# One ring tile, a combined load of the 5th and 6th tile, and a first tile stored in 8 and 24 KB pieces, in a contrast kernel

## The chip, the cores and the metric

The kernel runs on one core of a Trainium2 chip. The metric is device time in microseconds (us); lower is better. Most executions of one kernel agree within 0.3%. Positions in time are counted from the start of the profiled span, which is shorter than the device time by 2.2 us in most runs.

## The reference

The reference takes 48 images of 512 x 512 float32 values. It moves each image away from its own mean and clips:

```python
x: (16, 3, 512, 512) float32, factor = 1.5
mean = np.mean(x, axis=(2, 3), keepdims=True)
return np.clip(mean + factor * (x - mean), 0, 1)
```

Every value is read once and written once: 50.33 MB in, 50.33 MB out.

## The kernel before

The data are cut into 12 tiles of 128 rows of 32 KB (4 MB each, four images). A tile is loaded, summed (VectorE takes 4352 columns, ScalarE the other 3840), the sums become a bias by two small matmuls, and the tile is clipped in place, ScalarE then VectorE. SP (SyncE) issues the loads, ScalarE the stores, each into its own queue. A DMA has landed when its last byte is reported in place; the report goes to a semaphore, a counter that an engine waits for. Six buffers hold tiles, so the 7th tile is loaded when the first one has been stored.

```python
CHUNKS = (5120, 3072)
FIRST = (2048, 3072, 3072)
...
xpool = ctx.enter_context(tc.tile_pool(name="xpool", bufs=BUFS))      # BUFS = 6
...
def load(t):
    xt = xpool.tile([P, ROW], f32, name="xt")
    nc.sync.dma_start(out=xt, in_=dram(x_f, t))
    tiles[t] = xt

def compute(t):
    xt = tiles[t]
    ...                                     # sums on VectorE and ScalarE, matmuls, bias
    chunks, pieces = (FIRST, True) if t == 0 else (CHUNKS, False)
    c, done = 0, 0
    for n in chunks:
        part = xt[:, c : c + n]
        nc.scalar.activation(out=part, in_=part, func=Act.Relu, bias=bias, scale=factor)
        nc.vector.tensor_scalar(out=part, in0=part, scalar1=1.0, scalar2=None, op0=Alu.min)
        if pieces and c > 0:
            store(t, done, c)
            done = c
        c += n
    store(t, done, ROW)
...
for t in range(min(BUFS, n_tiles)):
    load(t)
for t in range(n_tiles):
    compute(t)
    if t + BUFS < n_tiles:
        load(t + BUFS)
```

The first tile leaves in three stores of 8, 12 and 12 KB per row; every other tile leaves in one store.

Of the kernel before, what the change touches and what calls it, by code (L numbers as in the profile page):

```python
# [1 line left out]

# [4 lines left out]


P = 128  # L10
ROW = 8192
BUFS = 6
CHUNKS = (5120, 3072)
FIRST = (2048, 3072, 3072)
SUM = 4352


@with_exitstack
def kernel(
    ctx: ExitStack,  # L20
    tc: tile.TileContext,
    x: bass.AP,
    factor: float,
    out: bass.AP,
):


    nc = tc.nc
    f32 = mybir.dt.float32
    Alu = mybir.AluOpType  # L30
    Act = mybir.ActivationFunctionType

    B, C, H, W = x.shape
    n_img, n_pix = B * C, H * W
    ppi = n_pix // ROW
    per_tile = P // ppi
    n_tiles = n_img // per_tile
    assert ppi * ROW == n_pix and per_tile * n_tiles == n_img

    factor = float(factor)  # L40
    wconst = (1.0 - factor) / float(n_pix)

    x_f = x.rearrange("b c h w -> (b c h w)")
    out_f = out.rearrange("b c h w -> (b c h w)")

    def dram(ap, t, c0=0, c1=ROW):
        return bass.AP(tensor=ap.tensor, offset=t * P * ROW + c0, ap=[[ROW, P], [1, c1 - c0]])

    consts = ctx.enter_context(tc.tile_pool(name="consts", bufs=1))
    xpool = ctx.enter_context(tc.tile_pool(name="xpool", bufs=BUFS))  # L50
    jpool = ctx.enter_context(tc.tile_pool(name="jpool", bufs=1))
    rpool = ctx.enter_context(tc.tile_pool(name="rpool", bufs=2))
    bpool = ctx.enter_context(tc.tile_pool(name="bpool", bufs=2))
    psum = ctx.enter_context(tc.tile_pool(name="psum", bufs=2, space=bass.MemoryType.PSUM))

    blockw = consts.tile([P, P], f32, name="blockw")
    nc.gpsimd.memset(blockw, 0.0)  # L57
    for a in range(0, P, ppi):
        nc.gpsimd.memset(blockw[a : a + ppi, a : a + ppi], wconst)  # L59

    tiles = {}

    def load(t):
        xt = xpool.tile([P, ROW], f32, name="xt")
        nc.sync.dma_start(out=xt, in_=dram(x_f, t))  # L65
        tiles[t] = xt

    def compute(t):
        xt = tiles[t]
        sums = rpool.tile([P, 2], f32, name="sums")  # L70
        nc.vector.tensor_reduce(  # L71
            out=sums[:, 0:1], in_=xt[:, 0:SUM], axis=mybir.AxisListType.X, op=Alu.add
        )
        junk = jpool.tile([P, ROW - SUM], f32, name="junk")
        nc.scalar.activation(  # L75
            out=junk, in_=xt[:, SUM:ROW], func=Act.Copy, accum_out=sums[:, 1:2]
        )
        pbias = psum.tile([P, 1], f32, name="pbias")
        nc.tensor.matmul(pbias, blockw, sums[:, 1:2], start=True, stop=False)  # L79
        nc.tensor.matmul(pbias, blockw, sums[:, 0:1], start=False, stop=True)  # L80
        bias = bpool.tile([P, 1], f32, name="bias")
        nc.vector.tensor_copy(out=bias, in_=pbias)  # L82

        chunks, pieces = (FIRST, True) if t == 0 else (CHUNKS, False)
        c, done = 0, 0
        for n in chunks:
            part = xt[:, c : c + n]
            nc.scalar.activation(out=part, in_=part, func=Act.Relu, bias=bias, scale=factor)  # L88
            nc.vector.tensor_scalar(out=part, in0=part, scalar1=1.0, scalar2=None, op0=Alu.min)  # L89
            if pieces and c > 0:  # L90
                store(t, done, c)
                done = c
            c += n
        store(t, done, ROW)

    def store(t, c0, c1):
        nc.scalar.dma_start(out=dram(out_f, t, c0, c1), in_=tiles[t][:, c0:c1])  # L97

    with tc.manual_schedule():
        for t in range(min(BUFS, n_tiles)):  # L100
            load(t)
        for t in range(n_tiles):
            compute(t)
            if t + BUFS < n_tiles:
                load(t + BUFS)


# [1 line left out]
_INS = ['x', 'factor']  # L109
_OUTS = [((16, 3, 512, 512), 'float32')]  # L110

_NUMBERS = {'factor': 1.5}


# [26 lines left out]
```

## Time and profile before

| | before |
|---|---|
| device time, median of 3 | 239.76 us (239.71 to 239.78) |
| span of the profile | 237.4 us |
| DMA: loads and stores, share of 16 engines | 49.6% + 49.2% |
| busy: ScalarE, VectorE | 55%, 47% |
| one tile on the compute engines | 14.6 us |
| last store issued | 210.1 us |

From the page of the kernel before: span, busy time of the engines, the two DMA rows of the 40 slices, and the DMA queues (packets, MB, share of 16 engines' span).

```profile
span 237.4 us, 310 instructions
PE 14.0 (6%) x48; PEld 12.0 (5%) x48; DVE 111.9 (47%) x49; ACT 131.1 (55%) x50; POOL 0.9 (0%) x9
...
DMA  7999998989999999999999999999999999999996
GB/s 265 442 442 442 420 446 374 472 384 455 453 425 409 409 436 442 442 442 442 442 442 425 436 398 421 442 442 442 442 442 436 442 425 392 425 442 442 442 442 265
...
q1 hardware_dynamic: 1728, 50.33, 49.6%
q10 hardware_dynamic: 2016, 50.33, 49.2%
```

The DMA row is 9 almost everywhere and the two queues add up to 98.8%: between the first packet and the last the 16 DMA engines hardly rest (by the packet records 0.1 us of 234.3), while both compute engines are idle about half of the time. One caution in reading the second row: a slice is 5.9 us long and 16 engines start a 32 KB packet nearly together, so a slice usually counts five such rounds, 442 GB/s, and sometimes four or six. The rate over 100 us and more is 431 to 433 GB/s.

The packet records of the trace give the size of each packet. One row of a tile is one packet: 32 KB in 1.213 us, 12 KB in 0.460 us, 8 KB in 0.309 us. 3072 packets of 1.213 us over 16 engines are 232.9 us, which is the floor for this form of transfer. The other 6.9 us of the 239.76 are, from the trace of before: 2.3 us outside the span (the median less the span of the profile), 1.8 us to the first packet, 1.2 us of slower packets and 1.3 us after the last packet, with small change.

From the timeline of before, the starts of the reductions of the 5th, 6th and 12th tile, and the last store (columns: start, duration, engine, line, operation, and in brackets the idle time before it and what ended it).

```profile
71.73 4.68 DVE L71 TENSOR_REDUCE sums<-xt 128x1 f32<-128x4352 f32 x1
86.36 4.68 DVE L71 TENSOR_REDUCE sums<-xt 128x1 f32<-128x4352 f32 x1
...
195.38 4.69 DVE L71 TENSOR_REDUCE sums<-xt 128x1 f32<-128x4352 f32 x1 [4.63 <-DMA xt<-in_x_dram]
...
210.11 0.34 ACTq L97 DMA_DIRECT2D out_dram<-xt  x1
```

Tiles follow each other on the compute engines at 14.6 us where they need not wait for data, and at about 19.4 us later, which is the time the DMA needs for one load and one store of 4 MB. At 210.1 us the last store is issued, but its first packet starts at 225.9 us in the packet records: older stores are ahead of it for 15.8 us. That number is the slack of the compute engines at the end.

One more line, from the waits of the DMA-issuing queue of before (total, times, longest, in us): SP could not issue the sixth load (at 22.77 us) before the second had landed (22.75 us): in the trace both count on the same semaphore.

```profile
SPq L65 <- DMA xt<-in_x_dram: 19.6, 1, 19.6
```

### The profile page before, as it was taken

What the parts mean: (1) busy time and instruction counts of PE and PEld (TensorE: products, weight loads), DVE (VectorE), ACT (ScalarE), POOL (GpSimd) and SP (SyncE); (2) the same over time, 40 slices, a digit from 0 to 9 for tenths busy, and PEclk for the clock granted to TensorE, in tenths of its full rate; (3) what the DMA queues carried; (4) which work ended last, traced back from release to release, by engine and by line L of the source; (5) the groups of instructions that cost most, each with busy time, mean ns of one, the idle gap of its engine ahead of it and who ended that gap; (6) DMA issues with size and microseconds to landing.
All of it is one profiled execution on the core that took longest, in us unless ns stands there. A gap on an engine that the chain in (4) does not pass through costs nothing.

```text
span 237.4 us, 310 instructions
## 1 busy us (share of the span) xinstructions
PE 14.0 (6%) x48; PEld 12.0 (5%) x48; DVE 111.9 (47%) x49; ACT 131.1 (55%) x50; POOL 0.9 (0%) x9
## 2 busy tenths in 40 slices
PE   0000010100101001010010010001001001000000
PEld 0000010100101001010010010001001001000000
DVE  0072855919468293782664372552734627330000
ACT  2058678586775967769279059256536806900000
POOL 1000000000000000000000000000000000000000
DMA  7999998989999999999999999999999999999996
GB/s 265 442 442 442 420 446 374 472 384 455 453 425 409 409 436 442 442 442 442 442 442 425 436 398 421 442 442 442 442 442 436 442 425 392 425 442 442 442 442 265
DMA packets 3745, 100.67 MB, mean 424 GB/s; under 512 B 416, under 2 KB 416, under 8 KB 416
## 3 DMA queue, kind: packets, MB, share of 16 engines
q1 hardware_dynamic: 1728, 50.33, 49.6%
q10 hardware_dynamic: 2016, 50.33, 49.2%
q14 instruction: 1, 0.01, 0.0%
HBM read 50.33 MB, written 50.33 MB: 424 GB/s over the span
## 4 chain that ended last, share of the span: by engine, by line
DMA 39%; another core or an unknown queue 24%; DVE 12%; ACT 10%; issue 2%; PE 1%; SPq 0%; ACTq 0%
DMA xt<-in_x_dram 19%; DMA out_dram<-xt 19%; ACT xt L88 9%; DVE xt L89 6%; DVE sums L71 5%; ACT junk L75 1%; PE pbias L80 1%; SPq L65 0%; PE pbias L79 0%; DVE bias L82 0%; ACTq L97 0%; ACTq L88 0%; ACTq L75 0%
## 5 line engine op out<-in xcount | busy, mean ns | idle before, releaser
L88 ACT ACTIVATE xt<-xt,bias 128x3072 f32<-128x3072 f32 (+2 forms) x25 | 87.9, 3563 | 21.0 <-DVE bias L82 13.7
L89 DVE TENSOR_SCALAR xt<-xt 128x3072 f32<-128x3072 f32 (+2 forms) x25 | 54.3, 2208 | 56.1 <-ACT xt L88 56.1
L71 DVE TENSOR_REDUCE sums<-xt 128x1 f32<-128x4352 f32 x12 | 56.2, 4683 | 33.9 <-DMA xt<-in_x_dram 33.9
L75 ACT ACTIVATE junk<-xt 128x3840 f32<-128x3840 f32 x12 | 40.8, 3402 | 55.4 <-DMA xt<-in_x_dram 41.9
L79 PE MATMUL pbias<-sums,blockw 128*128 128x1 f32 x24 | 7.0, 361 | 183.8 <-ACT junk L75 183.8
L79 PEld LDWEIGHTS pbias<-sums,blockw 128*128 128x128 f32 x24 | 6.0, 311 | 184.7 <-ACT junk L75 168.0
L80 PE MATMUL pbias<-sums,blockw 128*128 128x1 f32 x24 | 7.0, 362 | 2.9 <-DVE sums L71 2.5
L80 PEld LDWEIGHTS pbias<-sums,blockw 128*128 128x128 f32 x24 | 6.0, 312 | 3.9 <-DVE sums L71 3.4
L82 DVE COPY bias<-pbias 128x1 f32<-128x1 f32 x12 | 1.9, 158 | 8.2 <-PE pbias L80 8.2
L75 ACT ACTIVATION_READ_ACCUMULATOR junk<-xt 128x1 f32 x12 | 2.2, 186 | 0.0
L75 ACT ACT_TABLE_LOAD x1 | 1.3, 1283 | 0.7 <-PEq L122 0.7
L59 POOL MEMSET blockw<- 32x32 f32 x4 | 0.5, 117 | 0.2
L57 POOL MEMSET blockw<- 128x128 f32 x1 | 0.2, 204 | 0.3 <-POOLq L122 0.3
L122 POOL MEMSET const-bfloat16-1.0<- 128x1 bf16 x1 | 0.1, 111 | 0.0
L122 POOL MEMSET const-uint8-127<- 128x1 uint8 x1 | 0.1, 111 | 0.0
L122 POOL MEMSET const-float32-1.0<- 128x1 f32 x1 | 0.1, 108 | 0.0
L122 POOL MEMSET const-float32-0.0<- 128x1 f32 x1 | 0.1, 103 | 0.2 <-issue 0.2
## 6 DMA issues: line engine op xcount, KB each, us to landing
xt<-in_x_dram SPq DMA_DIRECT2D x12, 4096.0 KB, 33.9
out_dram<-xt ACTq DMA_DIRECT2D x11, 4096.0 KB, 50.6
out_dram<-xt ACTq DMA_DIRECT2D x2, 1536.0 KB, 31.1
out_dram<-xt ACTq DMA_DIRECT2D x1, 1024.0 KB, 15.5
```

The lines of the kernel that those rows point to most:

```text
L57: nc.gpsimd.memset(blockw, 0.0)
L59: nc.gpsimd.memset(blockw[a : a + ppi, a : a + ppi], wconst)
L71: nc.vector.tensor_reduce(out=sums[:, 0:1], in_=xt[:, 0:SUM], axis=mybir.AxisListType.X, op=Alu.add)
L75: nc.scalar.activation(out=junk, in_=xt[:, SUM:ROW], func=Act.Copy, accum_out=sums[:, 1:2])
L79: nc.tensor.matmul(pbias, blockw, sums[:, 1:2], start=True, stop=False)
L80: nc.tensor.matmul(pbias, blockw, sums[:, 0:1], start=False, stop=True)
L82: nc.vector.tensor_copy(out=bias, in_=pbias)
L88: nc.scalar.activation(out=part, in_=part, func=Act.Relu, bias=bias, scale=factor)
L89: nc.vector.tensor_scalar(out=part, in0=part, scalar1=1.0, scalar2=None, op0=Alu.min)
L122: nc = _bacc.Bacc("TRN2", target_bir_lowering=False, num_devices=1)
```

## The change

The six buffers become one tile with six places, so that one DMA can fill two of them. The 5th and 6th tile are loaded by one such DMA. The first tile is stored in two pieces, 8 and 24 KB per row, instead of three. The aim is fewer DMAs and fewer waits on reused semaphores.

```diff
-    xpool = ctx.enter_context(tc.tile_pool(name="xpool", bufs=BUFS))
+    xpool = ctx.enter_context(tc.tile_pool(name="xpool", bufs=1))
...
+    ring = xpool.tile([P, BUFS, ROW], f32, name="ring")
-    def load(t):
-        xt = xpool.tile([P, ROW], f32, name="xt")
-        nc.sync.dma_start(out=xt, in_=dram(x_f, t))
-        tiles[t] = xt
+    def load(t, c0=0, c1=ROW, n=1):
+        b = t % BUFS
+        src = bass.AP(
+            tensor=x_f.tensor,
+            offset=t * P * ROW + c0,
+            ap=[[ROW, P], [P * ROW, n], [1, c1 - c0]],
+        )
+        nc.sync.dma_start(out=ring[:, b : b + n, c0:c1], in_=src)
...
-            if pieces and c > 0:
-                store(t, done, c)
-                done = c
+            if t == 0 and c == FIRST[0]:
+                store(t, 0, c)
             c += n
-        store(t, done, ROW)
+        store(t, FIRST[0] if t == 0 else 0, ROW)
...
-        for t in range(min(BUFS, n_tiles)):
-            load(t)
+        load(0)
+        load(1)
+        load(2)
+        load(3)
+        load(4, n=2)
```

More of the change, by code (lines that the diff above doesn't have):

```diff
@@ L59 @@
         nc.gpsimd.memset(blockw[a : a + ppi, a : a + ppi], wconst)
-    tiles = {}
-    def load(t):
-        xt = xpool.tile([P, ROW], f32, name="xt")
-        nc.sync.dma_start(out=xt, in_=dram(x_f, t))
-        tiles[t] = xt
+    ring = xpool.tile([P, BUFS, ROW], f32, name="ring")
[7 more added lines that the diff above has]
+        nc.sync.dma_start(out=ring[:, b : b + n, c0:c1], in_=src)
     def compute(t):
-        xt = tiles[t]
+        xt = ring[:, t % BUFS, :]
         sums = rpool.tile([P, 2], f32, name="sums")
@@ L82, in compute @@
         nc.vector.tensor_copy(out=bias, in_=pbias)
-        chunks, pieces = (FIRST, True) if t == 0 else (CHUNKS, False)
-        c, done = 0, 0
-        for n in chunks:
+        c = 0
+        for n in FIRST if t == 0 else CHUNKS:
             part = xt[:, c : c + n]
@@ L89, in compute @@
             nc.vector.tensor_scalar(out=part, in0=part, scalar1=1.0, scalar2=None, op0=Alu.min)
-            if pieces and c > 0:
-                store(t, done, c)
-                done = c
+            if t == 0 and c == FIRST[0]:
+                store(t, 0, c)
             c += n
-        store(t, done, ROW)
+        store(t, FIRST[0] if t == 0 else 0, ROW)
     def store(t, c0, c1):
-        nc.scalar.dma_start(out=dram(out_f, t, c0, c1), in_=tiles[t][:, c0:c1])
+        nc.scalar.dma_start(out=dram(out_f, t, c0, c1), in_=ring[:, t % BUFS, c0:c1])
     with tc.manual_schedule():
-        for t in range(min(BUFS, n_tiles)):
-            load(t)
+        load(0)
[3 more added lines that the diff above has]
+        load(4, n=2)
         for t in range(n_tiles):
```

## The prediction

> **What bounds it now.** The 16 DMA engines. In the table of queues the loads (q1) take 49.6% and the stores (q10) 49.2% of 16 engines' span: 98.8% of 237.4 us is 234.6 us. In the 40 slices the DMA row is 9 in nearly all; only the first and last slice move less (265 GB/s against about 442). The trace's packets are one row each: 32 KB in 1.213 us, the 12 KB pieces in 0.460, the 8 KB pieces in 0.309. 3072 rows of 32 KB over 16 engines are 232.9 us: that is the floor, and 239.76 us lies 6.9 us above it, almost all of it launch, first packet and last receipt. ACT is busy 55%, DVE 47%; one tile costs them 14.6 us in series (starts of the reduction in the timeline), while a load and a store of a tile cost the DMA about 19.4 us.
>
> **What the change does.**
> 1. One ring instead of six buffers: same bytes, same instruction order; no work added.
> 2. Loads 5 and 6 as one DMA. No load reuses a semaphore then, so SP's 19.6 us wait for load 2 (waits of the DMA queue) goes. The load queue was not empty meanwhile, so this is worth nothing. But both tiles are released together, only when 8 MB have landed.
> 3. First tile stored as 8 + 24 KB instead of 8 + 12 + 12: 128 data packets fewer. A 24 KB packet should take about 0.91 us (estimate from 0.460 for 12 KB), which saves 0.1 us in all.
>
> The Trainium skill, "DMA: Bandwidth & Descriptors", section "Queues, rings and completion order", says each engine takes turns between its queues packet by packet. This trace agrees: in the second third of the span load and store packets are about equal in number. So a 24 KB piece gets more of the engine beside 32 KB loads than two 12 KB ones: the first tile's store should land about 10 us sooner (51 instead of 62 us), and loads later. Estimate by stepping such turns with the durations above (it reproduces before's landings to about 2 us): tile 5 becomes ready at 85 to 90 us instead of 60, so its reduction starts at 85 to 90 instead of 71.7: ACT and DVE idle there some 15 us. Compute then catches up (14.6 against 19.4 us), the last load lands at about 202 to 206 instead of 195 us, and the last store is issued at 217 to 221 instead of 210 us.
>
> **Critical path.** None of it, as long as either queue has packets: two earlier stores, over 5 us of work (before: about 17), are still queued when the last store is issued.
>
> **Prediction: 239.5 us, 8 times in 10 between 238.9 and 240.3.** Faster by over 2%: 0.02; within 2%: 0.94; slower by over 2%: 0.04.
>
> **What would show it.** DMA share again 98 to 99%, all middle slices 9; q10 with 144 packets fewer, q1 with 16 fewer; a new DMA wait of 10 to 18 us before the reduction of the 5th tile, none before the 6th; first store pieces landing near 51 us; SP's 19.6 us wait gone; last store issued later, landing at the same time.
>
> **What would make it wrong.** If the combined load uses fewer than 16 engines or smaller packets; if the later release of tile 5 lets both queues run dry together (an idle slice); if the last store comes after the backlog is gone (each us late is a us lost); if piece sizes change the packet rate more than I count.

## The result, and the profile after

| | before | after |
|---|---|---|
| device time, median of 6 | 239.77 us (239.71 to 240.00) | 239.66 us (239.51 to 240.13) |
| span of the profile | 237.4 us | 237.8 us |
| DMA shares, loads + stores | 49.6% + 49.2% | 49.7% + 49.1% |
| 5th tile's reduction starts | 71.7 us | 87.5 us |
| last store issued | 210.1 us | 218.9 us |

The ratio is 0.9997, 95% interval 0.9984 to 1.001: the two are the same.

The same lines of the page, for the kernel after:

```profile
span 237.8 us, 306 instructions
PE 14.0 (6%) x48; PEld 12.0 (5%) x48; DVE 111.8 (47%) x49; ACT 131.1 (55%) x50; POOL 0.9 (0%) x9
...
DMA  7999999999999999999999999999999999999996
GB/s 265 441 441 441 416 447 375 419 456 440 441 408 425 425 425 441 441 441 441 436 436 441 425 419 425 419 442 441 441 441 430 436 441 430 419 430 419 436 441 265
...
q1 hardware_dynamic: 1712, 50.33, 49.7%
q10 hardware_dynamic: 1872, 50.33, 49.1%
```

The load queue has 16 packets fewer and the store queue 144 fewer. The 16 are the completion packets of one load (one per engine); the 144 are 128 rows and 16 completions of one store. The bytes and the shares are what they were. That exactly 16 are gone also shows that the combined load still runs on 16 engines.

From the timeline of after, the reductions of the 5th, 6th and 12th tile and the last store:

```profile
87.54 4.68 DVE L77 TENSOR_REDUCE sums<-ring 128x1 f32<-128x4352 f32 x1 [15.70 <-DMA ring<-in_x_dram]
102.17 4.68 DVE L77 TENSOR_REDUCE sums<-ring 128x1 f32<-128x4352 f32 x1
...
204.17 4.69 DVE L77 TENSOR_REDUCE sums<-ring 128x1 f32<-128x4352 f32 x1 [4.64 <-DMA ring<-in_x_dram]
...
218.91 0.34 ACTq L100 DMA_DIRECT2D out_dram<-ring  x1
```

VectorE sits idle for 15.7 us until the combined load has landed, starts the 6th tile right behind the 5th, and issues the last store 8.8 us later than before. None of it reaches the time: the first packet of the last store starts at 226.0 us (225.9 before), because older stores were still being moved until then. The wait of SP for a load is gone from the waits of its queue, where only the waits for stores are left:

```profile
SPq L72 <- DMA out_dram<-ring: 149.2, 7, 36.1
```

From the DMA issues of after (size, median us from issue to landing):

```profile
ring<-in_x_dram SPq DMA_DIRECT2D x1, 8192.0 KB, 84.8
out_dram<-ring ACTq DMA_DIRECT2D x1, 3072.0 KB, 28.3
```

The 24 KB piece was issued at 28.0 us, so the first tile's store landed at 56.3 us. The 7th load, which waits for it, was issued at 56.4 us after against 64.4 us before.

### The profile page after: what moved, and what is told of

Its sections match the earlier page's. It is cut to its first block, busy times and chain, and to the rows that moved or that the text cites. A ratio compares the mean times of both kernels' runs of the same rounds, so it can differ in the third digit from the quotient of the medians. Undisturbed runs are those within 1.5% of the kernel's fastest.

```text
span 237.8 us, 306 instructions
## 1 busy us (share of the span) xinstructions
PE 14.0 (6%) x48; PEld 12.0 (5%) x48; DVE 111.8 (47%) x49; ACT 131.1 (55%) x50; POOL 0.9 (0%) x9
## 3 DMA queue, kind: packets, MB, share of 16 engines
q1 hardware_dynamic: 1712, 50.33, 49.7%
q10 hardware_dynamic: 1872, 50.33, 49.1%
## 4 chain that ended last, share of the span: by engine, by line
DMA 42%; DVE 22%; ACT 17%; another core or an unknown queue 7%; PE 2%; issue 2%; ACTq 0%; SPq 0%
DMA ring<-in_x_dram 26%; DMA out_dram<-ring 16%; ACT ring L92 14%; DVE ring L93 12%; DVE sums L77 9%; ACT junk L81 3%; PE pbias L86 2%; PE pbias L85 0%; DVE bias L88 0%; ACTq L100 0%; ACTq L92 0%; ACTq L81 0%; SPq L72 0%
## 5 line engine op out<-in xcount | busy, mean ns | idle before, releaser
L92 ACT ACTIVATE ring<-ring,bias 128x3072 f32<-128x3072 f32 (+2 forms) x25 | 87.9, 3564 | 21.4 <-DVE bias L88 12.5
L93 DVE TENSOR_SCALAR ring<-ring 128x3072 f32<-128x3072 f32 (+2 forms) x25 | 54.3, 2208 | 56.1 <-ACT ring L92 56.1
L77 DVE TENSOR_REDUCE sums<-ring 128x1 f32<-128x4352 f32 x12 | 56.2, 4681 | 42.8 <-DMA ring<-in_x_dram 42.8
L81 ACT ACTIVATE junk<-ring 128x3840 f32<-128x3840 f32 x12 | 40.8, 3402 | 63.8 <-DMA ring<-in_x_dram 48.2
L81 ACT ACTIVATION_READ_ACCUMULATOR junk<-ring 128x1 f32 x12 | 2.2, 186 | 0.0
```

What stands on the lines that cost most here:

```text
L77: nc.vector.tensor_reduce(out=sums[:, 0:1], in_=xt[:, 0:SUM], axis=mybir.AxisListType.X, op=Alu.add)
L81: nc.scalar.activation(out=junk, in_=xt[:, SUM:ROW], func=Act.Copy, accum_out=sums[:, 1:2])
```

## The experiments

The theory is that the time is the work of the DMA engines from first to last packet. What the change does to the moments at which tiles become ready is free as long as one of the two queues has a packet. The rivals are that gains and losses of the parts cancel, and that late tiles do cost time but by an amount hidden in something else. Eleven kernels were run; every result was correct. Where a loss is read below, its interval lies well clear of 1.

### Each part alone

`e1_ring_only`: the ring with six single loads and three pieces.

```diff
-            if t == 0 and c == FIRST[0]:
-                store(t, 0, c)
+            if t == 0 and c > 0:
+                store(t, done, c)
+                done = c
             c += n
-        store(t, FIRST[0] if t == 0 else 0, ROW)
+        store(t, done, ROW)
...
-        load(4, n=2)
+        load(4)
+        load(5)
```

> The ring alone: six single loads, first tile in 8 + 12 + 12 KB as before. Theory (the time is the DMA engines' packet work, and no part of the change touches it): 239.7 us, trace like before: SP's wait of about 19.6 us for load 2 is back, last store issued at about 210 us, no DMA wait before the 5th tile. Rival (a gain of one part is cancelled by a loss of another): at least one of the three runs with one part alone differs from before by 1 us or more, and two of them in opposite directions.

Measured: 239.65 us against 239.62 us of before on that chip; ratio 1.0004 (0.9989 to 1.0019). SP's wait for a load is back (19.4 us), the 5th reduction starts at 71.6 us, the last store is issued at 210.2 us. The single tile as such changes nothing.

`e2_pair_only`: the changed kernel with the store half of that edit alone (three pieces, the combined load kept).

> Ring and combined load, three pieces. Theory: 239.7 us; the 5th tile's reduction starts at 78 to 80 us (71.7 before), since the first tile's store lands near 62 us as before and the loads get their larger share; the 6th follows 14.6 us later; the slack at the end comes back: last load at about 195 us and last store issued at about 210 us. So the lost slack at the end belongs to the pieces, not to the combined load. Rival: the late release of the 5th tile costs time, 1 us or more above before.

Measured: 239.69 us; ratio 1.0003 (0.9988 to 1.0018). From its timeline:

```profile
77.87 4.68 DVE L77 TENSOR_REDUCE sums<-ring 128x1 f32<-128x4352 f32 x1 [5.87 <-DMA ring<-in_x_dram]
...
209.15 0.34 ACTq L101 DMA_DIRECT2D out_dram<-ring  x1
```

The combined load holds the 5th tile up by 5.9 us (its start is 0.1 us before the expected 78 to 80), and the last store is issued 1.0 us earlier than before.

`e3_pieces_only`: the changed kernel with the load half of that edit alone (single loads, 8 + 24 KB).

> Ring and 8 + 24 KB pieces, loads single. Theory: 239.6 us; first tile's store lands near 54 us; the 5th tile's reduction is not held up (about 72 us), the 6th waits for its load until about 87 us; last store issued at about 219 us as in the changed kernel, which shows that the pieces alone move the end. Rival: the fewer, larger packets gain 1 us or more below before.

Measured: 239.63 us; ratio 1.0002 (0.9987 to 1.0017). From its timeline, the reduction of the 6th tile and the last store:

```profile
88.63 4.69 DVE L77 TENSOR_REDUCE sums<-ring 128x1 f32<-128x4352 f32 x1 [2.25 <-DMA ring<-in_x_dram]
...
219.92 0.34 ACTq L100 DMA_DIRECT2D out_dram<-ring  x1
```

The pieces alone delay the later loads and the end: the last store is issued at 219.9 us, the 5th tile is not held up (71.7 us). So the two parts act in different places. The 15.7 us gap of the changed kernel is the combined load on top of loads that the pieces have slowed. And since all three variants are nominally within 0.05% of before, with intervals of 0.15% (0.4 us) to each side, no part has an effect of the 1 us that the rival asked for, and there is nothing of that size to cancel. The rival falls.

### How much slack the end has

The last tile gets one or two more reductions of its own columns, whose results nobody uses (4.68 us each, on VectorE ahead of the real one):

```diff
+        if t == n_tiles - 1:
+            for _ in range(1):          # 2 in the other three kernels
+                spare = rpool.tile([P, 1], f32, name="spare")
+                nc.vector.tensor_reduce(
+                    out=spare, in_=xt[:, 0:SUM], axis=mybir.AxisListType.X, op=Alu.add
+                )
         nc.vector.tensor_reduce(
             out=sums[:, 0:1], in_=xt[:, 0:SUM], axis=mybir.AxisListType.X, op=Alu.add
         )
```

`e4_after_tail1`: the changed kernel with one.

> The changed kernel with one more reduction of 4.68 us on the last tile's path. Theory: the last store is issued 4.7 us later (at about 223.6 us) and still finds about 1 us of older stores queued (in the changed kernel the first packet of the last store started at 226.0 us, 7.1 us after its issue): 239.7 us, at most 0.5 us longer. Rival (the end of the last tile's work is on the critical path): 4.7 us longer.

`e5_after_tail2`: the changed kernel with two.

> The same with two more reductions (9.4 us). Theory: the slack of 5 to 6 us is used up, 243 to 244 us, with a gap in the DMA row just before the last store's packets. Rival (on the critical path): 249.1 us. Rival (never matters): 239.7 us.

`e6_before_tail2`: the kernel before with two.

> The kernel before with the same two reductions (9.4 us). Theory: its slack is about 14 us (last store issued at 210.1 us, its first packet at 225.9 us), so 239.8 us, no change; the change has thus spent some 9 us of hidden slack that its time does not show. Rival: the same loss as in the changed kernel.

`e7_pair_tail2`: the combined load with three pieces, and two.

> Ring and combined load with three pieces, and the two reductions. Theory (the pieces, not the combined load, took the slack): 239.8 us, no change. Rival (the combined load took it): 243 to 244 us as in the changed kernel.

| kernel | last store issued, us | time, us | ratio to before (95%) |
|---|---|---|---|
| before, same chip | 210.1 | 239.73 | 1 |
| one more, after | 223.3 | 239.38 | 0.9982 (0.9965 to 0.9999) |
| two more, after | 227.9 | 241.72 | 1.0078 (1.0061 to 1.0095) |
| two more, before | 219.4 | 239.40 | 0.9981 (0.9966 to 0.9996) |
| two more, combined load and three pieces | 218.3 | 239.47 | 0.9986 (0.997 to 1.0002) |

(The issue times are of the profiled runs, that of before from its own profile.) Three of the four kernels with added work are nominally 0.1 to 0.2% faster. Added work can't be the reason; the runs of before on that chip spread from 239.54 to 240.37 us, and differences of this size are not read here.

The windows of the changed kernel between 226 and 229 us, then those of the same kernel with two more reductions (columns: window, length, busy us of PE, weight load, VectorE, ScalarE and GpSimd, granted clock, DMA share, GB/s):

```profile
226.00:229.00 3.00, 0.00 (x0) 0.00 (x0) 0.00 (x0) 0.00 (x0) 0.00 (x0) 1.00 1.06 459
```

```profile
226.00:229.00 3.00, 0.00 (x0) 0.00 (x0) 1.91 (x2) 0.12 (x1) 0.00 (x0) 1.00 0.41 175
```

With 9.0 us of delay the DMA engines stand idle before the last store's packets, and 2.0 us of the 9.0 appear in the time. In the two profiles the last packet ends 2.2 us later; 9.0 minus 2.2 gives a slack of 6.8 us. I had expected a loss of 3.5 to 4 us, because I had taken more than a microsecond from the 7.1 us for the latency of an issue to an idle queue; that latency was 0.84 us, and in the packet records what an engine loses depends on when that engine ends the older store, which is anywhere between 226.0 and 226.8 us. Before has at least 9.3 us of slack, and the kernel with the combined load and three pieces at least 9.1 us: it is the pieces that spend it. The changed kernel is as fast and more fragile.

### Where a combined load does cost time

The theory must also say when the change would have been harmful. `e8_load5` loads tiles 2 to 6 in one DMA of 20 MB:

```diff
-        load(1)
-        load(2)
-        load(3)
-        load(4, n=2)
+        load(1, n=5)
```

> The changed kernel with tiles 2 to 6 in one load (20 MB, released together). Theory (a late release is free as long as one queue has packets, and costs exactly the time in which both are empty): tile 2 is ready only near 70 us, loads and stores run dry together in the middle, 245 to 249 us, one or two slices of the DMA row at 1 to 7 in the middle. Rival (a combined load costs nothing, because all bytes are moved anyway): 239.7 us and no idle slice.

Measured: 249.72 us; ratio 1.043 (1.0413 to 1.0448). From its page and from its waits (total, times, longest):

```profile
DMA  7999999999999097989999999999999999999995
GB/s 297 445 434 429 404 434 392 441 409 462 429 424 424 0 424 291 387 387 445 429 434 424 424 424 424 445 450 445 429 436 424 424 424 424 440 445 450 429 440 254
```

```profile
DVE sums L77 <- DMA ring<-in_x_dram: 57.1, 2, 43.9
```

Tile 2 is ready at 71.9 us. At 81 us everything loaded is in, the only free place (tile 1's) has been refilled, and no second store has been issued: for 6.3 us no packet moves, then 1.4 us again at 97 us. Counted per engine, 8.5 us are idle in the middle. VectorE waited 43.9 us for the load, but the time grew by 10.1 us only: the wait is not the cost, the idle DMA is. My range (245 to 249) was exceeded by 0.7 us; the packets themselves also took 1.2 us more than in the changed kernel, most of it in loads just after the gap.

`e8_load4` combines tiles 3 to 6 (`load(1)`, then `load(2, n=4)`).

> The changed kernel with tiles 3 to 6 in one load (16 MB). Theory: tile 3 is ready near 80 us; loads and stores both run dry for about 2.4 us (estimate by stepping the turns, which gave 8.1 us for five tiles in one load, where 8.5 us were measured as idle and 10 us as time), so 242 to 244 us, with a dip in the DMA row near 95 to 110 us. Rival (any combined load of more than two tiles costs in proportion to the delay of the first of them: 10 us for five): 247 us or so; rival (free up to four): 239.7 us.

Measured: 244.50 us; ratio 1.0201 (1.0186 to 1.0216). From its page:

```profile
DMA  7999999999999999996999999999999999999994
GB/s 276 433 433 433 407 432 401 455 439 449 433 433 433 433 433 433 433 433 173 433 433 433 433 433 401 433 433 433 433 435 433 433 433 433 433 433 433 433 433 206
```

The dip is just after the stretch where it was expected (no packet moves from 110.0 to 111.4 us), and the packet records put the idle time at 2.0 us (expected 2.4). The time is 0.5 us above my range: the slow packets cost 1.9 us more than in the changed kernel. Why loads beside stores are sometimes slower than 1.213 us I have not found out; in before and after they add 1.2 and 1.6 us in all. Both rivals (free up to four, or in proportion to the delay, 247 us) are further off.

### Does the number of packets matter?

`e9_small_packets` gave each row of loads and stores as four runs of 8 KB, in the kernel with the pieces alone.

```diff
-            ap=[[ROW, P], [P * ROW, n], [1, c1 - c0]],
+            ap=[[ROW, P], [2048, 4], [1, 2048]],
         )
-        nc.sync.dma_start(out=ring[:, b : b + n, c0:c1], in_=src)
+        nc.sync.dma_start(out=ring[:, b, :].rearrange("p (k c) -> p k c", c=2048), in_=src)
...                                              # the stores in the same way
```

> The kernel with the pieces alone (single loads), with every load and store given as 8 KB runs, four to a row, in the same DMAs with the same waits. Theory (time is the sum of packet times): 3072 rows over 16 engines at 4 x 0.309 instead of 1.213 us are 4.4 us more, so 244 us, DMA row still 9 throughout, 12288 data packets. If the runs are joined again to 32 KB packets, 239.7 us and 3200 data packets, and the question stays open. Rival (packet size has no cost of its own): 239.7 us with 12288 packets.

Measured: 240.17 us; ratio 1.001 (0.9992 to 1.0027). Nothing was tested: neighbouring runs were joined again, and the packet records have 3200 data packets, as in `e3_pieces_only`. So this was a repetition of that kernel.

`e10_runs_of_8kb` keeps the runs apart by reversing their order in SBUF:

```diff
-            offset=t * P * ROW + c0,
-            ap=[[ROW, P], [P * ROW, n], [1, c1 - c0]],
+            offset=t * P * ROW + ROW - 2048,
+            ap=[[ROW, P], [-2048, 4], [1, 2048]],
...                                              # the stores in the same way
```

> As the last small-packet try (pieces alone, single loads, same DMAs and waits), but the four 8 KB runs of a row are kept apart by holding them in reversed order in SBUF, so that they cannot be joined (the result is still right: the sum takes them in another order, the stores reverse them again). 12288 data packets expected. Theory (time is the sum of packet times): 4 x 0.309 instead of 1.213 us a row is 4.4 us more over 3072 rows and 16 engines, so 244 us, DMA row 9 throughout. Rival (the number of packets costs nothing of its own, bytes alone count): 239.7 us. If packets of 8 KB next to each other run faster or slower than 0.309 us, the time follows that figure.

Measured: 244.62 us; ratio 1.0209 (1.0192 to 1.0226), with 12288 data packets. Its queues, and its windows near the end:

```profile
q1 hardware_dynamic: 6336, 50.33, 49.5%
q10 hardware_dynamic: 6352, 50.33, 49.1%
```

```profile
215.00:224.00 9.00, 1.18 (x4) 1.00 (x4) 4.84 (x2) 6.80 (x3) 0.00 (x0) 1.00 1.01 426
224.00:231.00 7.00, 0.00 (x0) 0.00 (x0) 4.51 (x2) 4.01 (x2) 0.00 (x0) 1.00 0.65 276
```

The total agrees with my 244 us, but not for my reason. In the steady part (70 to 200 us, bytes of the packet records) the rate fell from 433.1 to 428.1 GB/s, 1.2%, which over 233 us is an estimate of 2.7 us, not 4.4. The records of 8 KB overlap a little (the packet times between 70 and 200 us add up to 101.0% of 16 engines' time, against 100.2% in `e3_pieces_only`), so their sum overstates the cost. The other half is in the second window: the last store is issued at 229.8 us, after the backlog is gone, and 2.5 us of engine time are idle. In this kernel the first tile's pieces leave as runs of 8 KB beside loads of 8 KB, so the order of landings has moved too. What holds for this kernel is: going from 32 to 8 KB cost about 1.2% of the rate. Scaled from the 9088 packets more to the 128 fewer of the change, that is an estimate of 0.04 us, below anything a run here can show.

## Why the prediction was right

- **Bound.** Right. DMA share 98.8% in both profiles, and each of the parts alone left the time alone. Only the account of the 6.9 us above the floor was incomplete: "launch, first packet and last receipt" are 5.4 us of it (2.3 + 1.8 + 1.3), and the 1.2 us of slow packets were not seen.
- **The number.** 239.5 us predicted, 239.66 us measured. By itself this shows little, since any account in which the change costs nothing gives the same number; the positions below are the test. The 0.1 us that the pieces should save can't be seen. In the traces the sum of packet times even rose by 0.3 us, since the slower load packets happened to add 1.6 us instead of 1.2.
- **Turns between queues.** Right. Put in sequence by start and end, the packets of one engine in the steady part of the trace run load, store, load, store: in before, between 70 and 185 us, the kind changes in 1311 of 1503 steps. (The records do not name the engine; a packet was put to the engine whose last one ended just then.) This fits what the pieces alone showed, that the size of a store piece matters to the loads beside it. The size of the shift was off: I expected the first tile's store to land near 51 us, about 10 us sooner, and it landed at 56.3 us, 8 us sooner. My stepping had given a store 1.3 us from issue to first packet and 0.3 us from last packet to landing. Beside a full load queue the first piece took 3.5 us to its first packet (issued at 22.0, first packet at about 25.5 us), the second could only follow it (38.1 to 54.7 us), and its landing was reported 1.6 us after its last packet.
- **The late 5th tile.** Right: 87.5 us (85 to 90 predicted), a wait of 15.7 us (10 to 18), none before the 6th. SP's wait of 19.6 us went and was worth nothing, as said.
- **The end.** Last load and last store as predicted (204.2 and 218.9 us, in the ranges 202 to 206 and 217 to 221), and slack over 5 us. But the words "two earlier stores" were wrong: when the last store was issued, the 10th tile's store had ended at 217 us in the packet records and only the 11th was being moved. The 5 us were right, the picture of the queue was not. The prediction also did not separate the parts: the runs showed that the end is moved by the pieces (219.9 us alone) and not by the combined load (209.2 us alone).
- **What would make it wrong.** Two of the listed failures were produced on purpose: both queues dry (244.5 and 249.7 us) and the last store after the backlog (241.7 us). They set in where the theory put them, with times 0.5 to 1.3 us outside the expected ranges.

## What to carry to other kernels

This rests on one kernel on one core. Where transfers fill the DMA engines from first to last packet, as here, a change of buffers, issues or waits was worth nothing unless it changed bytes, packet rate, or a moment at which all queues are empty; look for idle slices first, not for waits. A long wait of a compute engine (43.9 us in one run) can cost much less than its length, and one of 15.7 us can cost nothing: ask how much older work is queued behind which it hides. And such a change can spend that slack without showing it in the time; adding a known piece of work at the end and seeing when the time moves is a cheap way to measure what is left.

## What the Trainium skill lacked or had wrong

- "DMA: Bandwidth & Descriptors", section "Queues, rings and completion order", has engines take turns between queues packet by packet, a packet being typically 9 to 17 descriptors. The turns are seen here, but a recorded packet was a single contiguous run (32, 24, 12 or 8 KB), and the turn changed after nearly each (1311 of 1503 steps in before).
- The same page, section "Bandwidth", lists a fabric ceiling of 435 GB/s and measures loads only (425 GB/s at 16 MB, issued from GpSimd). That section has no figure for loads and stores together from SP and ScalarE's queue (the nearest thing on the page is a row on copies between HBM tensors). Measured here: 433.1 GB/s in the steady part with 32 KB runs, 428.1 with 8 KB runs, on one core with nothing else running in this program.
- The same page, section "Latency and other measured facts", gives about 600 ns to the first byte for this kind of DMA. From the start of the issuing instruction, which itself takes 0.3 to 0.4 us, to the first recorded packet it was 1.0 us for the first load and 0.84 us for the last store of `e5_after_tail2` on idle engines. That does not contradict the page. But it was 3.5 us for the changed kernel's first store, issued beside a full load queue, and 3.8 us for a later one in `e8_load4` whose own queue was empty. One turn of a 32 KB load (1.2 us) on top of the 0.84 us is too short to explain it, and with loads of 8 KB runs it was again 3.5 us. No page was found that gives such a delay; its cause stays open.
- No page says that neighbouring runs in an access pattern are joined again before they become packets: four runs of 8 KB per row came out as 3200 data packets, and as 12288 when the runs were in reversed order on one side. Whether they are joined when the program is built or on the chip, the runs do not show.
- No page was found to give a cause for 32 KB load packets that take up to 2.9 us instead of 1.213 us at the start, beside stores, or after a gap (per engine 1.2 us in all in before, 3.5 us with four tiles in one load). It stays open.
